# Third pair's last Gram block first, two main-stream fills longer, last row factor by a square root on ScalarE

## The chip, the cores and the metric

The kernel runs on one core of one Trainium2 chip. The metric is the device time of one execution in microseconds (us). Before the change it is 1000.18 us, the median of 3 runs (999.9 to 1000.47).

## The reference, cut to what matters

One layer over 512 tokens with 16 learned tokens ahead of them, 2048 wide, all in float32:

```python
hn = _rmsnorm(h_res, norm_in_g[l])
P = hn @ w_in[l]                        # 2048 x (4224 + 4096)
# first 4224 columns: r, k, v, g_r (1024 each), two low-rank inputs; token-shifted
a = sigmoid(a0 + al @ a_lora_up); decay = exp(-exp(w_raw))
kk = k * k_k, divided by its norm in each head; k = k * (1 + (a - 1) * k_a)
# 16 heads x 64, step by step over the tokens:
S = S * w - (S kk) b^T + v k^T ;  y = S r
y_a = (groupnorm(y) + bonus) * silu(g_r)
# last 4096 columns: Bg, Cg, hc, g_c
y_b = Bg * causal_conv3(Cg * hc) * silu(g_c)
h_res = h_res + concat(y_a, y_b) @ w_out
out = _rmsnorm(h_res, norm_f_g)[:, 16:]
```

The last line is the one that the tail of the kernel computes: every row is scaled by one over the square root of its mean square plus a small constant, and by a gain for each column.

## The kernel before, in words

TensorE (PE) carries the kernel. The projection by `w_in` is a long **main stream** of matmuls (line 328, products `ps_k`, `ps_r`, `ps_v`, `ps_g`, `ps_C`, `ps_h`, `ps_B`, `ps_gc`). Each float32 product is made of three passes, with a coarse and a fine part of the weights (`w`) and of the inputs (`xh`, `xl`): a weight block arrives by DMA (`wr`, line 142), ScalarE (ACT) makes its coarse part (line 134), and VectorE (DVE) or GpSimd (POOL) its fine part (line 135). Weights lie in a ring of six buffers, the two banks of accumulators of the main stream in a ring too.

The state recurrence is done chunk by chunk (9 chunks, 64 tokens each but the first) for eight **pairs** of heads, i = 0 to 7. `prepare(i)` makes a pair's operands: decays and their running sums (`tz`, then the scan `cc`, then `e`), the scaled keys and receptances `bk` and `ar`, squares `sq`, and then the **Gram** matmuls (line 682): for each chunk c and each of two heads, `bk` against `ar`. Their results go to three kinds of accumulators: `za` holds chunks 0 to 3 (names `g_0_0`, `g_0_1` for the two heads in the order of instructions), `zc` chunks 4 to 7 (`g_4_0`, `g_4_1`), and `ze` chunk 8 alone (`g_8_0`, `g_8_1`). `ze` lies in the main stream's own ring of accumulators (tag "main"), so the main product that comes two buffers later can't start before `ze` has been read. DVE reads each by a multiplication with a mask into `gt` (line 692, helper `masked`): a piece of 128x512 for `za` and `zc`, of 128x128 for `ze`. After that the norms of the keys (`n_misc`, `n_tz`, lines 713 and 714) and the bonus sum (`zb`, lines 716 and 717) are computed on PE; `n_misc`, `n_tz` and `zb` take over the banks of `zc` and `za`.

The order on PE is written out by the program: `fill(ns)` places main matmuls, each counted as its columns times 0.43 ns, until `ns` are used up; between two fills stands the next special step. The table `FW` holds these amounts. On the other engines a scheduler of the framework orders the instructions, from the order of the program and its own estimates; an instruction's place on DVE, ACT, POOL and in the DMA queue of SyncE (SP) can move when a step moves on PE.

After the last pair has been solved, `fill(FW["begin"])` comes, and then the recurrence `recur`: it loads the operands of chunk 0 and 1 (`ct` from `opd`, line 936, 15 loads and one) and starts with the matmuls `rz` (line 957).

In the tail the output projection adds its last part to the rows (`end`, matmul line 1449; addition line 1453), ACT squares and sums it (line 1229, an activation and a read of its accumulator), `row_scale` adds the sum to what is there (line 1399) and takes the power -1/2 on POOL (line 98), and `finish_last` scales the four column blocks of the last 128 rows on DVE, ACT and POOL (lines 1418, 1420, 1422, 1423) and sends them out. Rows are handled in four groups t of 128; group 1 is the last.

Of the kernel before, what the change touches and what calls it, by code (L numbers as in the profile page):

```python
# [12 lines left out]
AF = mybir.ActivationFunctionType  # L13
# [12 lines left out]
NCH = SEQ // CH + 1  # L26
# [15 lines left out]

FW = dict(
    evac=34, start=1062, lora=2200, gram=8000, gram_b=13500, gram2=5500, misc=2000, v=2000, vt=1000, solve=24500, solve_first=30000,
    tr=3200, lev=3000, cp=4200, out=1500, begin=20300, p=2900, u=2900, s=4800, last=3700, mix=2600,
)


# [29 lines left out]
def hymba_kernel(ctx: ExitStack, tc: tile.TileContext, xt, xtok, front, w_in, w_out, pv, lup, cst, msk, gf, out):  # L78
    nc = tc.nc
    ctx.enter_context(tc.manual_schedule(engines={mybir.EngineType.PE}))  # L80
    cp = ctx.enter_context(tc.tile_pool(name="cp", bufs=1))
# [12 lines left out]
    def col(off, i=0):  # L94
        return pvt[:, off + i : off + i + 1]

    def rsqrt(y, v):
        nc.gpsimd.tensor_tensor(out=y, in0=v, in1=mhalf[:, 0 : v.shape[1]], op=ALU.pow)
# [198 lines left out]
    with tc.issue_after(head):  # L297
        nc.vector.tensor_scalar(
            out=omm, in0=pvt[:, V_MU : V_MU + 33], scalar1=-1.0, scalar2=1.0, op0=ALU.mult, op1=ALU.add
        )  # L300
        for d, off in (
# [4 lines left out]
                out=d, in0=pvt[:, off : off + 8], scalar1=0.5, scalar2=None, op0=ALU.mult  # L306
            )
        nc.vector.tensor_scalar(
            out=hv[:, 4], in0=pvt[:, V_KA : V_KA + 8], scalar1=-0.5, scalar2=1.0, op0=ALU.mult, op1=ALU.add
# [232 lines left out]
    def step():  # L542
        t = next(flow, None)
        if t is None:
            run_pending(float("inf"))
        else:
            clock[0] += t
            run_pending(clock[0])
        return t

    def fill(ns):
        while ns > 0:
            seen = len(ready)
            t = step()
            if t is None:
                return
            ns -= t
            if len(ready) > seen:
                ns += FW["evac"]
# [26 lines left out]
    def c3(t):  # L586
        return t.rearrange("p (c s) -> p c s", s=CH)
# [39 lines left out]
    def prepare(i):  # L627
        p = i % 2
# [21 lines left out]
            out=bk[:, :, 1], in0=c3(k), scalar=hv[:, 2, i : i + 1], in1=c3(te), op0=ALU.mult, op1=ALU.mult  # L650
        )
        nc.gpsimd.tensor_scalar(
            out=ta, in0=ta, scalar1=hv[:, 3, i : i + 1], scalar2=hv[:, 4, i : i + 1], op0=ALU.mult, op1=ALU.add
        )
        nc.vector.scalar_tensor_tensor(
            out=ar[:, :, 0], in0=c3(k), scalar=col(V_KK, i), in1=e1[:, :, 0:CH], op0=ALU.mult, op1=ALU.mult
# [7 lines left out]
        r = got["r", i]  # L664
        nc.vector.tensor_tensor(
            out=ar[:, 1:NCH, 1], in0=c3(r), in1=e1[:, 1:NCH, 1 : CH + 1], op=ALU.mult
        )
        nc.vector.scalar_tensor_tensor(
            out=r, in0=r, scalar=hv[:, 5, i : i + 1], in1=ta[:, CH:LP], op0=ALU.mult, op1=ALU.mult
# [6 lines left out]
        shift = {0: 2000, 1: 2500, 3: 6000}.get(i, 0)  # L676
# [3 lines left out]
        def gram(z, c, c0):  # L680
            for h, hs, ho in heads:
                nc.tensor.matmul(  # L682
                    z[h][:, c - c0],
                    bk[hs, c, h : h + 2, :].rearrange("p a s -> p (a s)"),
                    ar[hs, c].rearrange("p a s -> p (a s)"),
                    start=True, stop=True,
                )

        def masked(z, c0, c1):
            with ahead():  # L690
                for h in range(2):
                    nc.vector.tensor_tensor(  # L692
                        out=gt[:, h, c0:c1],
                        in0=z[h],
                        in1=gmask[:, h].unsqueeze(1).to_broadcast([P, c1 - c0, P]),
                        op=ALU.mult,
                    )


        za = [pz.tile([P, 4, P], F32, tag="tz", name=f"g{i}_0_{h}") for h in range(2)]  # L700
        zc = [pi.tile([P, 4, P], F32, tag=("misc", "ser")[h], name=f"g{i}_4_{h}") for h in range(2)]
        ze = [pm.tile([P, 1, P], F32, tag="main", name=f"g{i}_8_{h}") for h in range(2)]
        for c in range(NCH):
            gram((za, zc, ze)[c // 4], c, c // 4 * 4)
        for z, a, b in ((ze, 8, 9), (za, 0, 4), (zc, 4, 8)) if i == 2 else ((za, 0, 4), (zc, 4, 8), (ze, 8, 9)):
            masked(z, a, b)
        fill(FW["gram2"] - shift + 1300 * (i == 1) + 2000 * (i == 3))

        n2 = tr(f"n2{i}")
        zn = [pool.tile([2, 288], F32, tag=t, name=f"n2_{i}_{t}") for pool, t in ((pi, "misc"), (pz, "tz"))]  # L710
# [58 lines left out]
        for m in (2, 4, 8):  # L769
            for b in range(16 // (2 * m)):  # L770
# [4 lines left out]
                    out=pq,  # L775
# [5 lines left out]
                    out=tq.rearrange("p (i j) -> p i j", i=m), in_=pq, op=ALU.add, axis=AX.X  # L781
                )
                nc.vector.tensor_tensor(
                    out=pq,
# [30 lines left out]
        v = got["v", i]  # L815
# [245 lines left out]
    for i in range(0, NPAIR, 2):  # L1061
        invert([prepare(i), prepare(i + 1)])
# [9 lines left out]
    mix = [pp.tile([P, 4, SEQ], F32, tag=f"R{m}", name=f"mix{m}") for m in range(4)]  # L1072
# [87 lines left out]
    ssq = pw.tile([P, 92], F32, name="ssq")[:, 0:20].rearrange("p (a b) -> p a b", b=5)  # L1160
    fv = pw.tile([P, 4, 3], F32, name="fv")
# [56 lines left out]
    def here(t, n):  # L1218
        return xa[t][:, n * 512 : (n + 1) * 512] if n < 2 else xb[n - 2][:, t]
# [11 lines left out]
    def gain(t, n, eng, o=slice(0, 512)):  # L1231
        h = here(t, n)[:, o]
        eng.tensor_tensor(out=h, in0=h, in1=gfb[:, n * 512 : (n + 1) * 512][:, o], op=ALU.mult)
# [95 lines left out]
    for half in range(2):  # L1329
        for g in range(4):  # L1330
            b, m1, m2 = U[half, "P5", g], U[half, "M1", g], U[half, "M2", g]
# [39 lines left out]
    z = {}  # L1371
# [17 lines left out]
    def row_part(t, n):  # L1389
        w = fv[:, t, 0:1]  # L1390
        nc.vector.tensor_reduce(out=w, in_=ssq[:, t, 0:n], op=ALU.add, axis=AX.X)
        nc.vector.tensor_scalar(out=w, in0=w, scalar1=RMS_EPS, scalar2=None, op0=ALU.add)

    scales = {}

    def row_scale(t, n, eng=nc.gpsimd):
        f = fv[:, t]
        w, v, r = f[:, 0:1], f[:, 1:2], f[:, 2:3]
        eng.tensor_scalar(out=v, in0=ssq[:, t, n : n + 1], scalar1=w, scalar2=None, op0=ALU.add)
        rsqrt(r, v)  # L1400
        scales[t] = r
# [13 lines left out]
    def finish_last(t):  # L1415
        r = scales[t]
        o = out[t * P : (t + 1) * P]
        nc.vector.tensor_scalar(out=here(t, 2), in0=here(t, 2), scalar1=r, scalar2=1.0, op0=ALU.mult, op1=ALU.mult)
        nc.sync.dma_start(o[:, 1024:1536], here(t, 2))
        nc.scalar.activation(here(t, 0), here(t, 0), AF.Copy, scale=r)  # L1420
        nc.scalar.dma_start(o[:, 0:512], here(t, 0))
        nc.gpsimd.tensor_scalar(out=here(t, 3), in0=here(t, 3), scalar1=r, scalar2=1.0, op0=ALU.mult, op1=ALU.mult)
        nc.vector.tensor_scalar(out=here(t, 1), in0=here(t, 1), scalar1=r, scalar2=1.0, op0=ALU.mult, op1=ALU.mult)
        nc.sync.dma_start(o[:, 512:1024], here(t, 1))
        nc.scalar.dma_start(o[:, 1536:DM], here(t, 3))

    with tc.manual_schedule(engines={mybir.EngineType.DVE, mybir.EngineType.Activation, mybir.EngineType.Pool}):
        end = po.tile([P, 512], F32, tag="o", name="end")
        for g in range(4):
            product((1, "M2", g), [end], (0,))  # L1430
        for t in (2, 3):
            row_part(t, 3)
            row_scale(t, 3)
        row_part(0, 3)
        row_part(1, 3)
        finish(2, (2, 0, 3))
        finish(3, (2,))
        nc.vector.tensor_tensor(out=here(0, 2), in0=here(0, 2), in1=end, op=ALU.add)
        squares(0, 2)
        row_scale(0, 3)  # L1440
        finish(3, (0, 3))
        gain(1, 3, nc.vector)
        ends = [po.tile([P, 256], F32, tag="o", name=f"end{part}") for part in range(2)]
        for part in range(2):
            cols = slice(256 * part, 256 * part + 256)
            for jj in range(8):
                hi, lo = right[(1, "M2", jj // 2), jj % 2]
                for n, (m, w) in enumerate(((0, hi), (0, lo), (1, hi))):
                    nc.tensor.matmul(
                        ends[part], left("M2", jj, m, 1), w[:, cols], start=(jj == 0 and n == 0), stop=(jj == 7 and n == 2)  # L1450
                    )
            h = here(1, 2)[:, cols]
            nc.vector.tensor_tensor(out=h, in0=h, in1=ends[part], op=ALU.add)
            squares(1, 2, part)
            if part == 0:
                gain(1, 2, nc.vector, cols)
                finish(0, (2, 0))
                nc.vector.tensor_tensor(out=fv[:, 1, 0:1], in0=fv[:, 1, 0:1], in1=ssq[:, 1, 3:4], op=ALU.add)
        finish(0, (3,))
        row_scale(1, 4, nc.vector)  # L1460
        gain(1, 2, nc.vector, slice(256, 512))
        finish_last(1)


# [61 lines left out]
```

## Time and profile before

| | |
|---|---|
| median of 3 runs | 1000.18 us (999.9 to 1000.47) |
| the profiled execution's own time | 999.89 us |
| its span | 998.0 us |
| granted TensorE clock, mean | 0.998 |
| busy: PE / DVE / ACT / POOL | 986.7 / 689.2 / 412.2 / 271.6 us |
| DMA moved | 179.48 MB, mean 180 GB/s |

The span is the time that the profiled execution covers; its own time is 1.89 us longer, and the median of the runs is 0.29 us above that. A row of the timeline gives start, duration, engine, line, operation, result and operands, shape and count; in brackets stand the idle time of the engine ahead of it and what ended it. PE is busy nearly all of the time, so the rows to look for are those with a bracket on PE, and those behind its last matmul.

### The profile page before, as it was taken

Reading aid. Unit: us, or ns where it says so; the run is one execution under the profiler, and the core shown is the slowest. Engines: PE = TensorE matmul, PEld = TensorE weight load, DVE = VectorE, ACT = ScalarE, POOL = GpSimd, SP = SyncE. Lnnn points to the kernel's source line nnn. Section 1 sums busy time; section 2 is a strip of 40 time slices with the busy share of each in tenths; the row PEclk is TensorE's granted clock in tenths of the full one; section 3 lists DMA queues with packets and bytes.
Section 4 is the critical chain, followed back from the end, with each engine's and each line's share of the span. In section 5 each row is a group of like instructions: output and inputs, shape, how many; then the busy total and the mean of one; then the engine's idle time right before and its main releaser. Section 6 shows DMA issues by size and latency. Waiting matters only on the chain.

```text
span 998.0 us, 22792 instructions
## 1 busy us (share of the span) xinstructions
PE 986.7 (99%) x9211; PEld 910.8 (91%) x9211; DVE 689.2 (69%) x1314; ACT 412.2 (41%) x770; POOL 271.6 (27%) x286
## 2 busy tenths in 40 slices
PE   9999999999999999999999999999999999999996
PEld 8999999999998999998999998989889898888885
DVE  7777975487774579735579735246555598999895
ACT  7554432343523535232534232233332326645553
POOL 0122423133422324222324222223242423011001
PEclk9999999999999999999999999999999999999999
DMA  9527585437584365854265954978783698798634
GB/s 324 160 79 184 122 224 144 119 106 179 128 215 140 95 180 130 230 145 111 85 180 120 232 143 114 347 266 283 223 266 96 169 266 232 230 293 224 144 99 168
DMA packets 184985, 179.48 MB, mean 180 GB/s; under 512 B 112176, under 2 KB 141616, under 8 KB 184368
## 3 DMA queue, kind: packets, MB, share of 16 engines
q1 hardware_dynamic: 182288, 169.12, 58.2%
q0 software_dynamic: 2304, 8.39, 4.8%
q8 instruction: 72, 1.18, 0.5%
q10 hardware_dynamic: 288, 0.52, 0.1%
q14 instruction: 33, 0.27, 0.1%
HBM read 139.28 MB, written 38.71 MB: 178 GB/s over the span
## 4 chain that ended last, share of the span: by engine, by line
PE 95%; DMA 2%; DVE 1%; issue 1%; POOL 0%; ACT 0%; DVEq 0%; SPq 0%; POOLq 0%
PE ps_g L328 9%; PE ps_r L328 9%; PE ps_h L328 9%; PE ps_gc L328 9%; PE ps_B L328 9%; PE ps_v L328 9%; PE ps_C L328 8%; PE ps_k L328 8%; PE M L1242 8%; PE P L1242 4%; PE Q L1242 2%; PE g L682 2%; DMA ct<-opd 1%; PE ps_lora L328 1%; PE rz L957 1%; PE zs L1004 1%
## 5 line engine op out<-in xcount | busy, mean ns | idle before, releaser
L134 ACT CAST w<-wr 128x512 fp32r<-128x512 f32 x252 | 153.4, 619 | 280.0 <-PE ps_h L328 47.4
L135 POOL TENSOR_TENSOR w<-wr,w 128x512 fp32r<-128x512 f32 x119 | 168.2, 1415 | 365.2 <-ACT w L134 326.7
L135 DVE TENSOR_TENSOR w<-wr,w 128x512 fp32r<-128x512 f32 x133 | 98.3, 743 | 98.6 <-ACT w L134 97.6
L328 PE MATMUL ps_r<-xh,w 128*128 128x256 f32 (+1 forms) x512 | 95.2, 282 | 1.0 <-DVE gt L692 1.0
L328 PE MATMUL ps_k<-xh,w 128*128 128x256 f32 (+1 forms) x512 | 95.4, 284 | 0.0
L328 PE MATMUL ps_v<-xh,w 128*128 128x272 f32 (+1 forms) x512 | 95.4, 284 | 0.0
L328 PE MATMUL ps_h<-xh,w 128*128 128x258 f32 (+1 forms) x512 | 93.1, 281 | 0.0
L328 PE MATMUL ps_C<-xh,w 128*128 128x258 f32 (+1 forms) x512 | 92.5, 281 | 0.0
L328 PE MATMUL ps_g<-xh,w 128*128 128x258 f32 (+1 forms) x512 | 91.7, 280 | 0.0
L328 PE MATMUL ps_B<-xh,w 128*128 128x512 f32 x256 | 83.1, 394 | 0.0
L328 PEld LDWEIGHTS ps_r<-xh,w 128*128 128x128 f32 x512 | 80.2, 189 | 1.6 <-DVE gt L692 1.2
L328 PE MATMUL ps_gc<-xh,w 128*128 128x512 f32 x256 | 81.6, 393 | 0.0
L328 PEld LDWEIGHTS ps_k<-xh,w 128*128 128x128 f32 x512 | 80.3, 189 | 0.3
L328 PEld LDWEIGHTS ps_v<-xh,w 128*128 128x128 f32 x512 | 80.1, 189 | 0.3
L328 PEld LDWEIGHTS ps_h<-xh,w 128*128 128x128 f32 x512 | 79.5, 189 | 0.3
L328 PEld LDWEIGHTS ps_C<-xh,w 128*128 128x128 f32 x512 | 79.2, 189 | 0.6
L328 PEld LDWEIGHTS ps_g<-xh,w 128*128 128x128 f32 x512 | 79.2, 189 | 0.2
L328 PE MATMUL ps_k<-xl,w 128*128 128x256 f32 (+1 forms) x256 | 73.0, 285 | 0.0
L328 PE MATMUL ps_v<-xl,w 128*128 128x256 f32 (+1 forms) x256 | 72.5, 283 | 0.0
L328 PE MATMUL ps_h<-xl,w 128*128 128x256 f32 (+1 forms) x256 | 72.5, 283 | 0.0
L328 PE MATMUL ps_g<-xl,w 128*128 128x256 f32 (+1 forms) x256 | 72.4, 283 | 0.0
L328 PE MATMUL ps_r<-xl,w 128*128 128x256 f32 (+1 forms) x256 | 72.1, 282 | 0.0
(312 smaller groups left out, 2204.3 us busy)
## 6 DMA issues: line engine op xcount, KB each, us to landing
wr<-in_w_in_dram SPq DMA_DIRECT2D x126, 512.0 KB
ct<-opd SPq DMA_DIRECT2D x56, 320.0 KB
wo<-in_w_out_dram SPq DMA_DIRECT2D x21, 512.0 KB
opd<-gt SPq DMA_DIRECT2D x16, 576.0 KB
x<-in_w_out_dram POOLq DMA_DIRECT2D x16, 512.0 KB, 5.7
opd<-ar SPq DMA_DIRECT2D x8, 576.0 KB
opd<-bt SPq DMA_DIRECT2D x64, 64.0 KB
ct<-opd SPq DMA_DIRECT2D x16, 256.0 KB
```

Of the source, the lines that this page charges most:

```text
L134: nc.scalar.copy(hi, rq)
L135: low[q] = eng.tensor_tensor(out=lo, in0=rq, in1=hi.bitcast(F32), op=ALU.subtract).ins
L328: nc.tensor.matmul(ps[r], ww[:, w], xx[:, kt, a:b], start=(kt == 0 and n == 0), stop=(kt == KT - 1 and n == 2))
L682: nc.tensor.matmul(z[h][:, c - c0], bk[hs, c, h : h + 2, :].rearrange("p a s -> p (a s)"), ar[hs, c].rearrange("p a s -> p (a s)"), start= ...
L957: nc.tensor.matmul(z[e][ho if e else hs, 0, k], ct[e][hs, k, o : o + CH], uv(e, k, hs, h) if part else st[hs, 4 * e + k], start=(part == 0 ...
L1004: nc.tensor.matmul(zs[hs, j], bb[:, h], uv(e, k, everything, h), start=True, stop=True)
L1242: nc.tensor.matmul(bank[s], left(prod, jj, m, s), w, start=(jj == 0 and n == 0), stop=(jj == 7 and n == 2))
```

## The change

Four edits:

1. In `prepare`, for the third pair (i = 2), the Gram matmuls of chunk 8 (`ze`) come ahead of those of chunks 0 to 7, and the masks follow the same order. In the program of before, the masks of `ze` stood first for that pair already, and its matmuls last.
2. For the second pair (i = 1), the fill between Gram and norms grows by 400 (1300 to 1700).
3. The fill ahead of the recurrence grows by 500 (20300 to 20800).
4. The factor of the last row group is made by an activation Sqrt on ACT (with the sum as bias) and a reciprocal on DVE, in place of an addition on DVE and a power on POOL. The gain on the second half of the last block is moved ahead of it. After the factors of groups 2 and 3 an activation Sqrt on one element per row is added, whose result isn't used: it stands where the activation table of the square root is to be loaded.

```diff
-    tr=3200, lev=3000, cp=4200, out=1500, begin=20300, p=2900, u=2900, s=4800, last=3700, mix=2600,
+    tr=3200, lev=3000, cp=4200, out=1500, begin=20800, p=2900, u=2900, s=4800, last=3700, mix=2600,
...
-        for c in range(NCH):
-            gram((za, zc, ze)[c // 4], c, c // 4 * 4)
-        for z, a, b in ((ze, 8, 9), (za, 0, 4), (zc, 4, 8)) if i == 2 else ((za, 0, 4), (zc, 4, 8), (ze, 8, 9)):
+        blocks = [(za, 0, 4), (zc, 4, 8), (ze, 8, 9)]
+        if i == 2:
+            blocks = blocks[2:] + blocks[:2]
+        for z, a, b in blocks:
+            for c in range(a, b):
+                gram(z, c, a)
+        for z, a, b in blocks:
             masked(z, a, b)
-        fill(FW["gram2"] - shift + 1300 * (i == 1) + 2000 * (i == 3))
+        fill(FW["gram2"] - shift + 1700 * (i == 1) + 2000 * (i == 3))
...
         w, v, r = f[:, 0:1], f[:, 1:2], f[:, 2:3]
+        if eng is nc.scalar:
+            eng.activation(v, ssq[:, t, n : n + 1], AF.Sqrt, bias=w)
+            nc.vector.reciprocal(r, v)
+            scales[t] = r
+            return
         eng.tensor_scalar(out=v, in0=ssq[:, t, n : n + 1], scalar1=w, scalar2=None, op0=ALU.add)
...
             row_scale(t, 3)
+        nc.scalar.activation(fv[:, 1, 1:2], fv[:, 3, 0:1], AF.Sqrt)
         row_part(0, 3)
...
-        row_scale(1, 4, nc.vector)
         gain(1, 2, nc.vector, slice(256, 512))
+        row_scale(1, 4, nc.scalar)
```

Lines below the third edit of the file are numbered 4 higher in the changed program (713 becomes 717), and 9 or 10 higher in the tail (1229 becomes 1233, 1409 becomes 1418).

**Second pair, PE.** On PE around the norms (`n_`) and the bonus sum (`zb`) of the second pair, before the change:

```order
L328 MATMUL ps_g_1_1652<-xh,w_1482 128x258 x2
L713 MATMUL n_1_misc<-sq_h,ones 2x288
L714 MATMUL n_1_misc<-sq_l,ones 2x288
L713 MATMUL n_1_tz<-sq_h,ones 2x288
L714 MATMUL n_1_tz<-sq_l,ones 2x288
L716 MATMUL zb_1798<-rk_h,ones 128x512
L717 MATMUL zb_1798<-rk_l,ones 128x512
L328 MATMUL ps_g_1_1652<-xl,w_1482 128x258
L328 MATMUL ps_g_1_1652<-xh,w_1482 128x258
L328 MATMUL ps_C_0_1825<-xh,w_1545 128x256
```

and after it:

```order
L328 MATMUL ps_g_1_1652<-xh,w_1482 128x258 x2
L328 MATMUL ps_g_1_1652<-xl,w_1482 128x258
L328 MATMUL ps_g_1_1652<-xh,w_1482 128x258
L328 MATMUL ps_C_0_1812<-xh,w_1545 128x256
L328 MATMUL ps_C_0_1812<-xl,w_1545 128x256
L717 MATMUL n_1_misc<-sq_h,ones 2x288
L718 MATMUL n_1_misc<-sq_l,ones 2x288
L717 MATMUL n_1_tz<-sq_h,ones 2x288
L718 MATMUL n_1_tz<-sq_l,ones 2x288
L720 MATMUL zb_1823<-rk_h,ones 128x512
```

Four main matmuls have moved ahead of the norms, two of them already of the next product, `ps_C`.

**Third pair, DVE.** On DVE from the product `bk` (line 659) of the third pair to the mask of `g_8_0`, before (the masks of `g_4_1` and `g_8_1` follow; the subtraction `sq_l`, line 602, stands three rows ahead of the first row):

```order
L659 TENSOR_TENSOR bk_2657<-ta_2738,e_2816 128x9x64
L135 TENSOR_TENSOR w_2795<-wr_2793,w_2795 128x512
L668 SCALAR_TENSOR_TENSOR r_2624<-r_2624,hv,ta_2738 128x512
L729 STREAM_TRANSPOSE bt_3062<-bk_2657 128x512 x2
L602 TENSOR_TENSOR rk_l<-r_2624,rk_h 128x512
L821 STREAM_TRANSPOSE vs_3136<-v_2781 128x576
L135 TENSOR_TENSOR w_2858<-wr_2856,w_2858 128x512
L692 TENSOR_TENSOR gt_2919<-g_0_0_2920,cs 128x512
L692 TENSOR_TENSOR gt_2919<-g_0_1_2921,cs 128x512
L692 TENSOR_TENSOR gt_2919<-g_4_0_2922,cs 128x512
L692 TENSOR_TENSOR gt_2919<-g_8_0_2924,cs 128x128
```

and after:

```order
L659 TENSOR_TENSOR bk_2661<-ta_2742,e_2820 128x9x64
L135 TENSOR_TENSOR w_2795<-wr_2793,w_2795 128x512
L668 SCALAR_TENSOR_TENSOR r_2582<-r_2582,hv,ta_2742 128x512
L602 TENSOR_TENSOR sq_l<-sq_2834,sq_h 128x576
L733 STREAM_TRANSPOSE bt_3066<-bk_2661 128x512
L602 TENSOR_TENSOR rk_l<-r_2582,rk_h 128x512
L733 STREAM_TRANSPOSE bt_3066<-bk_2661 128x512
L825 STREAM_TRANSPOSE vs_3140<-v_2781 128x576
L135 TENSOR_TENSOR w_2858<-wr_2856,w_2858 128x512
L692 TENSOR_TENSOR gt_2923<-g_8_0_2928,cs 128x128
L692 TENSOR_TENSOR gt_2923<-g_8_1_2929,cs 128x128
L692 TENSOR_TENSOR gt_2923<-g_0_0_2924,cs 128x512
```

The mask of `g_8_0` has moved from the fourth place of the six to the first; and `sq_l`, which stood ahead of `bk`, now stands between `bk` and the masks. On POOL, ahead of that, the scaling of `tz` (line 639), on which the scan and everything after it rests, stands so before:

```order
L358 MEMSET pr_k_2969 128x1
L639 TENSOR_SCALAR tz_2675<-tz_2675 128x576
L135 TENSOR_TENSOR w_2637<-wr_2632,w_2637 128x512
L661 COPY dd<-e_2658 128x9
L642 MEMSET e_3150 128x9
```

and so after:

```order
L358 MEMSET pr_k_2969 128x1
L135 TENSOR_TENSOR w_2595<-wr_2590,w_2595 128x512
L639 TENSOR_SCALAR tz_2687<-tz_2687 128x576
L661 COPY dd<-e_2662 128x9
L642 MEMSET e_3154 128x9
```

The fine part of a weight block has moved ahead of `tz`. It is the block whose coarse part ACT makes behind its part of `tz` before (second half, line 578) and ahead of it after. On PE the Gram matmuls of this pair stand four main matmuls later than before.

**Recurrence, PE and SP.** The matmuls `rz` stand four main matmuls later than before; the loads of `ct` on SP keep their order and their neighbours.

**Tail, ACT and DVE.** On ACT, from the sums of squares of the first part (`sqj` of groups 3 and 1) on, after the change:

```order
L1233 ACTIVATE sqj_3_None,ssq<-xb_11533 128x512
L1233 ACTIVATE sqj_1_None,ssq<-xb_11533 128x512
L1443 ACT_TABLE_LOAD
L1443 ACTIVATE fv<-fv 128x1
L1233 ACTIVATE sqj_2_None,ssq<-xb_11508 128x512
L1421 ACTIVATE xa_11037<-xa_11037,fv 128x1024
```

This ACT_TABLE_LOAD is the only one besides the one at the start of the program (line 246), which before has alone; the sum of squares of group 2 follows it. At the end of DVE's program stand, before:

```order
L1453 TENSOR_TENSOR xb_11508<-xb_11508,end_12273 128x256
L1409 SCALAR_TENSOR_TENSOR xb_11533<-xb_11533,fv,gfb 128x512
L1399 TENSOR_SCALAR fv<-ssq,fv 128x1
L1300 TENSOR_TENSOR xb_11508<-xb_11508,gfb 128x256
L1418 TENSOR_SCALAR xb_11508<-xb_11508,fv 128x512
```

and after:

```order
L1463 TENSOR_TENSOR xb_11508<-xb_11508,end_12274 128x256
L1418 SCALAR_TENSOR_TENSOR xb_11533<-xb_11533,fv,gfb 128x512
L1304 TENSOR_TENSOR xb_11508<-xb_11508,gfb 128x256
L1405 RECIPROCAL fv<-fv 128x1
L1427 TENSOR_SCALAR xb_11508<-xb_11508,fv 128x512
```

The addition has left DVE, and the reciprocal stands between the gain and the last scalings.

## The prediction

> **What bounds the kernel now.** I read the page first: the busy times and the chain that ended last.
>
> ```profile
> PE 986.7 (99%) x9211; PEld 910.8 (91%) x9211; DVE 689.2 (69%) x1314; ACT 412.2 (41%) x770; POOL 271.6 (27%) x286
> PE 95%; DMA 2%; DVE 1%; issue 1%; POOL 0%; ACT 0%; DVEq 0%; SPq 0%; POOLq 0%
> ```
>
> PE is busy 986.7 of 998.0 us, and the change takes no matmul away. So there are only 11.3 us to win from, and the next view, PE's waits by what ended them, tells how much of that is waiting in the middle.
>
> ```profile
> PE ps_r L328 <- DVE gt L692: 1.0, 1, 1.0
> PE rz L957 <- DMA ct<-opd: 0.3, 1, 0.3
> ```
>
> Two of the edits aim at these two waits. The third wait that I look for is in PE's weight loads, and the last stretch begins where PE stops, at 989.83 + 0.28 = 990.11, 7.9 us before the end:
>
> ```profile
> 130.60 0.19 PEld L716 LDWEIGHTS zb<-rk_h,ones 128*128 128x128 f32 x1 [0.43 <-issue]
> 989.83 0.28 PE L1449 MATMUL end<-home,m 128*128 128x256 f32 x1
> ```
>
> All sums below go against the profiled execution, 999.89 us; the median of the runs, 1000.18, lies 0.29 above it, and I add this back at the end. A measurement of this kernel can tell about 0.2%, 2.0 us, from no change.
>
> **Third pair (edit 1).** The timeline of PE and DVE around the third pair's Gram:
>
> ```profile
> 214.60 2.28 PE L682 MATMUL g<-ar,bk 64*128 64x128 f32 x36
> 218.74 0.28 PE L328 MATMUL ps_k<-xl,w 128*128 128x272 f32 x1
> 218.87 0.29 PE L328 MATMUL ps_k<-xh,w 128*128 128x272 f32 x1
> 220.11 0.38 PE L328 MATMUL ps_r<-xh,w 128*128 128x256 f32 x1 [0.96 <-DVE gt L692]
> 217.99 2.87 DVE L692 TENSOR_TENSOR gt<-g,cs 128x512 f32<-128x512 f32 x6
> ```
>
> Main matmuls start 0.12 to 0.13 apart (218.74, 218.87), so `ps_r` was due at 218.99 and came at 220.11: **1.12 us** lost. It takes over the buffer of `ze`, whose mask is the fourth of the six: 217.99 plus three pieces of some 0.6 plus its own 0.27 is 220.06. Put first, that mask would end at 218.26, before 218.99, and all 1.12 would go. But DVE doesn't reach it at the same time as before:
>
> ```profile
> 198.43 0.48 ACT L578 ACTIVATE tz<-tz,hv 128x256 f32<-128x256 f32 x1 [1.53 <-PE tz L572]
> 198.98 0.62 ACT L134 CAST w<-wr 128x512 fp32r<-128x512 f32 x1
> 199.07 1.67 POOL L639 TENSOR_SCALAR tz<-tz 128x576 f32<-128x576 f32 x1 [3.21 <-ACT tz L578]
> 200.70 1.30 POOL L135 TENSOR_TENSOR w<-wr,w 128x512 fp32r<-128x512 f32 x1
> 209.31 1.86 DVE L658 TENSOR_TENSOR ta<-ta,k 128x576 f32<-128x576 f32 x1 [0.26 <-POOL ta L652]
> 211.09 0.74 DVE L602 TENSOR_TENSOR sq_l<-sq,sq_h 128x576 fp32r<-128x576 f32 x1
> 212.57 0.75 DVE L659 TENSOR_TENSOR bk<-ta,e 128x576 f32<-128x576 f32 x1
> 213.35 0.67 ACT L660 COPY bk<-bk 64x576 f32<-64x576 f32 x1 [2.85 <-DVE bk L659]
> ```
>
> By the order of instructions, the weight block's cast stands ahead of ACT's `tz` now and the block's fine part ahead of POOL's. The cast waits for a weight buffer that PE frees about where it freed it before, at some 198.9; then 0.62 for the cast, 1.30 for the fine part, and `tz` starts on POOL near 200.8 instead of 199.07: **1.75 late**. What of that reaches `bk` at line 659? Along the way 0.1 to 0.2 goes in idle time of DVE, and `sq_l`, which stood ahead of `bk`, no longer does (0.74, some 0.07 of it beside its neighbours). I take 0.8 late: `bk` at 213.35, ACT's copy done at 214.8. The Gram matmuls stand four main matmuls later, at 214.60 + 0.47 = 215.07, so they are covered by about 0.3 us.
>
> From `bk` to the first mask it took 217.99 - 212.57 = 5.42 us. Now `sq_l` lies in this stretch, +0.67. One step there was stretched before:
>
> ```profile
> 213.24 0.68 DVE L135 TENSOR_TENSOR w<-wr,w 128x512 fp32r<-128x512 f32 x1
> 216.98 1.08 DVE L135 TENSOR_TENSOR w<-wr,w 128x512 fp32r<-128x512 f32 x1
> 215.92 1.60 POOL L135 TENSOR_TENSOR w<-wr,w 128x512 fp32r<-128x512 f32 x1 [4.55 <-ACT w L134]
> ```
>
> The same operation takes 0.68 alone and 1.08 beside POOL's, which ran to 217.52; moved to about 218.3 it runs behind POOL's, -0.41. The first mask then starts at 213.35 + 5.42 + 0.67 - 0.41 = 219.03 and ends at 219.3, and `ps_r` waits some 0.35 instead of 1.12: **0.75 won**. Bounds: if the delay of `bk` is only 0.4 and POOL is out of the way, 1.1; if `bk` is 1.0 late and the two meet again, the mask ends at 219.9 and 0.2 is left. I take 0.75, nearest to the chain of rows.
>
> The Trainium skill ("SBUF — State Buffer", the section "SBUF: two separate sides") says that a DVE instruction with two SBUF inputs and a GpSimd instruction that reads SBUF exclude each other, whichever starts first. The trace agrees: behind 217.52 DVE's step had 0.54 left. By that rule a meeting would cost up to the whole rest of POOL's 1.30, and the term could fall to about zero; by the rows it fell by 0.4.
>
> **Second pair (edit 2).**
>
> ```profile
> 127.82 2.86 DVE L692 TENSOR_TENSOR gt<-g,cs 128x512 f32<-128x512 f32 x6
> 130.21 0.29 PE L714 MATMUL n_tz<-sq_l,ones 128*2 128x288 f32 x1
> 130.63 0.47 PE L716 MATMUL zb<-rk_h,ones 128*128 128x512 f32 x1
> ```
>
> `zb` follows `n_tz` by 0.42, where matmuls of this width start 0.13 apart, and its weight load was idle for 0.43: 0.29 lost. `zb` takes over the bank of `g_4_1`, the fifth mask, which ends at 127.82 + 2.0 + 0.67 = 130.49. With four main matmuls (0.47) ahead of the norms, `zb` is due at 130.81, 0.3 behind that. But `ps_C` now starts ahead of the norms, at 130.06, in the buffer of `g_8_0`, the fourth mask, done at 127.82 + 1.8 + 0.27 = 129.89: covered by 0.17. **0.29 won** (0 to 0.29).
>
> **Recurrence (edit 3).**
>
> ```profile
> 630.97 0.81 PE L957 MATMUL rz<-ct 64*64 64x64 f32 x28
> 632.11 0.33 PE L957 MATMUL rz<-ct 64*64 64x64 f32 x4 [0.33 <-DMA ct<-opd]
> ```
>
> The last load of chunk 0 landed 0.33 after PE wanted it. Four main matmuls more ahead of `rz` give 0.47, while the loads keep their place on SP behind the same weight load, which waits for a buffer that PE frees; so they keep their distance to PE. **0.33 won** (0.1 to 0.33, since the cover is only 0.14).
>
> **Tail (edit 4).**
>
> ```profile
> 2.03 0.20 ACT L246 ACTIVATE warm<-warm 128x1 f32<-128x1 f32 x1
> 990.98 0.19 ACT L1229 ACTIVATION_READ_ACCUMULATOR sqj<-xb 128x1 f32 x1
> 991.20 0.21 DVE L1399 TENSOR_SCALAR fv<-ssq,fv 128x1 f32<-128x1 f32 x1
> 991.33 0.41 DVE L1300 TENSOR_TENSOR xb<-xb,gfb 128x256 f32<-128x256 f32 x1
> 991.49 0.66 POOL L98 TENSOR_TENSOR fv<-fv,mhalf 128x1 f32<-128x1 f32 x1 [4.33 <-DVE fv L1399]
> 992.19 0.72 ACT L1420 ACTIVATE xa<-xa,fv 128x512 f32<-128x512 f32 x1 [1.02 <-POOL fv L98]
> L757 DVE RECIPROCAL nd<-nd x8: 249/249/251, 95.5 to 562.8; 72x16 f32<-72x16 f32 x8
> ```
>
> Now the square root follows the read at 991.17 on the same engine: 0.20 by the small activation, 0.3 with an allowance of 0.1, done by 991.5. The gain takes 0.41 from 991.20 on. The reciprocal starts near 991.6 and takes at most the 0.25 that 16 columns take, at least the 0.15 or so of a small step: done at 991.75, and the scalings start at 991.78 instead of 992.19. **0.42 won** (0.2 to 0.6).
>
> The price is the second table load. It lies here:
>
> ```profile
> 0.73 1.28 ACT L246 ACT_TABLE_LOAD   x1 [0.73 <-PEq L1513]
> 979.01 0.63 ACT L1229 ACTIVATE sqj_None<-xb 128x512 f32<-128x512 f32 x1 [1.07 <-DVE xb L1223]
> 985.18 0.63 ACT L1229 ACTIVATE sqj_None<-xb 128x512 f32<-128x512 f32 x1 [2.57 <-DVE xb L1438]
> 987.78 0.42 ACT L1229 ACTIVATE sqj<-xb 128x256 f32<-128x256 f32 x1 [0.84 <-DVE xb L1453]
> ```
>
> 1.28 + 0.20 go into an idle time of 1.07, so groups 2 and 3 run 0.4 to 0.5 late; the idle times of 2.57 and 0.84 behind them take that up before PE's last part, 987.27. Cost nothing; without this cover it would be 0.45.
>
> The Trainium skill ("ScalarE: Activation LUTs", the section "What ACT_TABLE_LOAD costs") counts a drain of about 1.38 us with each load, 2.66 in all. The one load in this trace shows 1.28 and the next instruction 0.02 behind it, but it had nothing to drain. By the page's price groups 2 and 3 would run 1.8 late and the last sum some 0.3: the tail would win 0.1, and the whole 0.3 less.
>
> **The sum.** 0.75 + 0.29 + 0.33 + 0.42 = 1.79. 999.89 - 1.8 = 998.1 for a profiled execution; 1000.18 - 1.8 = **998.4** for the median.
>
> **The rivals.**
> *All waits go* (the third pair's chain is hardly late): 1.1 + 0.29 + 0.33 + 0.45 = 2.2, 998.0. For it speaks that DVE and ACT have idle time in that chain; against it the 1.75 at its head.
> *The third pair stays as it was*: `bk` is later than I think. At over 1.05 late the Gram itself waits (copy done 214.02 + 1.05 = 215.07). With the whole 1.75 passed on and `sq_l` behind it, the mask ends at 218.26 + 1.75 + 0.67 = 220.7: the place loses 0.6 instead of winning, and the time is 1000.18 - 1.04 + 0.6 = 999.7. The head of the chain speaks for it; `sq_l` ahead of `bk`, which is gone, against it.
> *Slower: the second pair's solve starves.* Its divisors `nd` are now loaded from SP behind the 576 KB of `ar`, and DVE has the gating `g` ahead of them.
>
> ```profile
> 161.33 0.64 SPq L796 DMA_DIRECT2D xo<-sx  x1
> 171.64 0.70 DVE L845 STREAM_TRANSPOSE xn<-xT 128x512 f32<-128x512 f32 x1
> ```
>
> The solve's start is read back from DRAM by loads whose last is issued at 161.97; with an allowance of 2 to 3 for its landing and 171.64 for its use, some 7 us of cover are there. The delay is 576 KB at the page's mean of 180 GB/s, 3.3 us. From 7 on PE waits for each us; at 8.8 all is lost, and at 10.8 the kernel is 2 us slower, 1002.2. The distance speaks against it.
> *Edits 2 and 3 only move the waits* (`ps_C` waits for its mask, the `ct` loads come later by as much): 1.17 is won, 999.0.
>
> **How the numbers follow.** My forecast with its bounds has 0.50, all waits gone 0.17, the third pair unchanged or worse 0.15, moved waits 0.10, the slower case 0.08. The range is 997.6 to 999.9: from all waits gone with 0.6 in the tail, to the third pair's loss. Faster by over 0.2% means under 998.18: the first rival's 0.17, and 0.17 of the forecast's 0.50, together 0.34. Slower by over 0.2%: 0.08. Within: 0.58.
>
> **What would show it.** After: `ps_r` of the fourth pair with a bracket of about 0.2 to 0.4 for `gt`, POOL's `tz` some 1.7 us later against PE, no bracket on `g`; `zb` 0.13 behind `n_tz` in the second pair and none on `ps_C`; no bracket on `rz`; the last scalings 1.67 us behind PE's last matmul instead of 2.08. A new bracket on PE anywhere else, above all where the shifts of up to five main matmuls leave other steps earlier or later, would make me wrong, as would a table load longer than 1.9 us.

## The result, and the profile after

The changed kernel takes **997.8 us** (median of 12 runs, 997.26 to 998.39) against 1000.2 us for the kernel before, measured beside it (12 runs, 998.8 to 1000.79). The ratio is 0.9978 (95% interval 0.9971 to 0.9985), so 1.5 to 2.9 us were won. Measured again on another occasion the ratio was 0.9983 (0.9974 to 0.9991). The forecast was 998.4, a gain of 1.8.

The profiled execution took 998.33 us with a span of 996.5 (before: 999.89 and 998.0). The waits of PE after the change, by what ended them, are these two; both waits that were to go are gone, and one is new:

```profile
PE pwarm L187 <- DVE cold L184: 1.4, 1, 1.4
PE tz L571 <- DVE xT L923: 0.3, 1, 0.3
```

**Second pair.** PE, timeline: `zb` follows `n_tz` by 0.14 instead of 0.42, and the matmuls of `ps_C` ahead of the norms have no bracket.

```profile
130.33 0.33 PE L328 MATMUL ps_C<-xh,w 128*128 128x256 f32 x1
131.00 0.30 PE L718 MATMUL n_tz<-sq_l,ones 128*2 128x288 f32 x1
131.14 0.40 PE L720 MATMUL zb<-rk_h,ones 128*128 128x512 f32 x1
```

**Third pair.** PE and DVE after the change: `ps_r` follows `ps_k` by 0.12, so all of the 1.12 is gone. The masks begin at 218.05, both masks of `ze` are done by 218.52 (0.47 for the two), and `ps_r` was due at 219.27 and came then.

```profile
215.35 2.28 PE L682 MATMUL g<-ar,bk 64*128 64x128 f32 x36
219.15 0.29 PE L328 MATMUL ps_k<-xh,w 128*128 128x272 f32 x1
219.27 0.28 PE L328 MATMUL ps_r<-xh,w 128*128 128x256 f32 x1
217.47 0.64 DVE L135 TENSOR_TENSOR w<-wr,w 128x512 fp32r<-128x512 f32 x1
218.05 2.86 DVE L692 TENSOR_TENSOR gt<-g,cs 128x128 f32<-128x128 f32 x6
```

That is 1 us earlier than I had worked out (219.03), though the head of the chain came as late as I had said, and a little more. POOL and DVE after:

```profile
199.77 1.29 POOL L135 TENSOR_TENSOR w<-wr,w 128x512 fp32r<-128x512 f32 x1 [5.41 <-ACT w L134]
201.03 1.66 POOL L639 TENSOR_SCALAR tz<-tz 128x576 f32<-128x576 f32 x1
202.73 1.36 DVE L641 TENSOR_TENSOR_SCAN cc<-smask,tz 128x576 f32<-128x576 f32 x1 [5.44 <-POOL tz L639]
212.39 0.75 DVE L659 TENSOR_TENSOR bk<-ta,e 128x576 f32<-128x576 f32 x1
```

and the scan before, with the second pair's ahead of it:

```profile
100.48 2.43 DVE L641 TENSOR_TENSOR_SCAN cc<-smask,tz 128x576 f32<-128x576 f32 x1 [0.44 <-POOL tz L639]
200.78 2.43 DVE L641 TENSOR_TENSOR_SCAN cc<-smask,tz 128x576 f32<-128x576 f32 x1 [3.81 <-POOL tz L639]
```

POOL's `tz` came 1.96 later (201.03 against 199.07). But before the change POOL's weight step at 200.70 ran beside the scan and stretched it to 2.43 us; now that step lies ahead of `tz`, and the scan takes 1.36. The second pair's scan is the only other long one, and it too has a weight step of POOL beside it (100.41, 1.29 long). In all fourteen profiles every scan with such a step beside it takes 2.43 or 2.44, and every other one 1.34 to 1.36. The move gave 1.07 back at once. Another 0.40 was made up on the way to the step ahead of `bk` (line 658), and 0.67 because `sq_l` no longer lies ahead, so that `bk` came 0.18 earlier than before by the clock, not 0.8 later. From `bk` to the first mask it took 5.66, close to the 5.68 worked out.

**The new wait** lies ahead of all this, at the low-rank matmul of the third pair. PE and DVE after, then PE and DVE before:

```profile
195.44 0.40 PE L328 MATMUL ps_v<-xh,w 128*128 128x256 f32 x2
196.10 0.36 PE L571 MATMUL tz<-la,luh 128*128 128x272 f32 x1 [0.26 <-DVE xT L923]
192.96 1.25 DVE L372 SCALAR_TENSOR_TENSOR r<-pr_r,omm,sh_r 128x512 f32<-128x512 f32 x1 [0.84 <-ACT sh_r L371]
194.13 2.43 DVE L923 COPY xT<-z 32x128 f32<-32x128 f32 x8
```

```profile
195.25 0.29 PE L328 MATMUL ps_v<-xh,w 128*128 128x272 f32 x1
195.38 0.29 PE L571 MATMUL tz<-la,luh 128*128 128x272 f32 x1
192.52 2.40 DVE L919 COPY xT<-z 32x128 f32<-32x128 f32 x8 [0.22 <-PE z L913]
194.95 0.76 DVE L372 SCALAR_TENSOR_TENSOR r<-pr_r,omm,sh_r 128x512 f32<-128x512 f32 x1
```

DVE now makes `r` before it copies the solve's results out of the bank (`xT<-z`), and `tz`, which takes that bank over, waits for the copies. Counted from start to start, `tz` came 0.54 behind the last matmul of `ps_v` (195.44 + 0.12, then 196.10) where 0.12 to 0.13 is due: 0.42 lost, more than the bracket of 0.26.

**Recurrence.** `rz` runs through in one piece:

```profile
630.69 0.69 PE L961 MATMUL rz<-ct 64*64 64x64 f32 x32
```

From the last main matmul ahead of it to the first behind it 0.83 us pass, where it was 1.62 in the execution before. So that execution had lost 0.79 there, not the 0.33 of the bracket: 28 of the 32 matmuls stood under one row of 0.81 that already held some of the waiting.

**Tail.** ACT and DVE after:

```profile
975.85 1.28 ACT L1443 ACT_TABLE_LOAD   x1
977.25 0.62 ACT L1233 ACTIVATE sqj_None<-xb 128x512 f32<-128x512 f32 x1
989.26 0.19 ACT L1233 ACTIVATION_READ_ACCUMULATOR sqj<-xb 128x1 f32 x1
989.48 0.29 ACT L1404 ACTIVATE fv<-ssq,fv 128x1 f32<-128x1 f32 x1
989.82 0.16 DVE L1405 RECIPROCAL fv<-fv 128x1 f32<-128x1 f32 x1
990.01 0.72 ACT L1429 ACTIVATE xa<-xa,fv 128x512 f32<-128x512 f32 x1 [0.24 <-DVE fv L1405]
```

PE's last matmul ends at 988.39, 1.72 earlier than before, and the scalings start 1.62 behind it instead of 2.08. But from there to the end of the span it takes 996.5 - 990.01 = 6.49 us, where it took 998.0 - 992.19 = 5.81. The 0.46 won was given back, and 0.22 more. What lay there was the question of the last three experiments.

### The profile page after: what moved, and what is told of

Same layout as the page of the kernel before. It is cut to its first block, busy times and chain, and to the rows that moved or that the text cites. A ratio compares the mean times of both kernels' runs of the same rounds, so it can differ in the third digit from the quotient of the medians.

```text
span 996.5 us, 22799 instructions
## 1 busy us (share of the span) xinstructions
PE 986.5 (99%) x9211; PEld 911.1 (91%) x9211; DVE 686.7 (69%) x1314; ACT 413.4 (41%) x773; POOL 268.2 (27%) x285
## 4 chain that ended last, share of the span: by engine, by line
PE 98%; DVE 1%; ACT 0%; issue 0%; DVEq 0%; ACTq 0%
PE ps_k L328 9%; PE ps_h L328 9%; PE ps_r L328 9%; PE ps_C L328 9%; PE ps_g L328 9%; PE ps_gc L328 9%; PE ps_v L328 9%; PE ps_B L328 9%; PE M L1246 8%; PE P L1246 4%; PE Q L1246 2%; PE g L682 2%; PE ps_lora L328 1%; PE rz L961 1%; PE zs L1008 1%; PE zy L1012 1%
## 5 line engine op out<-in xcount | busy, mean ns | idle before, releaser
L328 PE MATMUL ps_C<-xl,w 128*128 128x256 f32 (+1 forms) x256 | 71.9, 281 | 0.0
```

Source lines behind the costliest of these rows:

```text
L328: nc.tensor.matmul(ps[r], ww[:, w], xx[:, kt, a:b], start=(kt == 0 and n == 0), stop=(kt == KT - 1 and n == 2))
```

## The experiments

One table first. All numbers are from PE's timeline, start to start, less what the same step takes without a wait (0.13 for `zb`, 0.12 for `tz` and `ps_r`, 0.83 for the first `rz` block), and at the end the two stretches behind PE's last matmul. All in us.

| kernel | zb | tz | ps_r | rz | PE's end to scalings | scalings to end |
|---|---|---|---|---|---|---|
| before | 0.29 | 0.01 | 1.12 | 0.79 | 2.08 | 5.81 |
| changed | 0.01 | 0.42 | 0 | 0 | 1.62 | 6.49 |
| e1_gram | 0.31 | 0 | 0 | 0.47 | 2.08 | 5.80 |
| e2_norms | 0 | 0.41 | 0.88 | 0.57 | 2.09 | 5.83 |
| e3_begin | 0.31 | 0 | 1.12 | 0.20 | 2.08 | 5.84 |
| e4_tail | 0.31 | 0.01 | 1.11 | 0.01 | 1.63 | 6.09 |
| after_again | 0 | 0.42 | 0 | 0.01 | 1.62 | 6.55 |
| e5_no_norms | 0.29 | 0 | 0 | 0 | 1.63 | 6.07 |
| e6_given_back | 0 | 0.01 | 0 | 0.04 | 1.63 | 6.53 |
| e8_begin_more | 0 | 0.01 | 0 | 0.01 | 1.63 | 6.37 |
| e7_no_warm | 0 | 0.43 | 0 | 0 | 2.89 | 6.13 |

The measured times are less sharp than these rows. In the eleven profiles of the table the first `ps_g` matmul, which lies ahead of every edit, starts anywhere from 104.34 to 105.61, because the start of the kernel varies. That alone is more than any one term.

**Each edit alone.** The four parts, each put into the kernel before:

```diff
--- before
+++ e1_gram
...
+        if i == 2:
+            blocks = blocks[2:] + blocks[:2]
+        for z, a, b in blocks:
+            for c in range(a, b):
+                gram(z, c, a)
...
--- before
+++ e2_norms
-        fill(FW["gram2"] - shift + 1300 * (i == 1) + 2000 * (i == 3))
+        fill(FW["gram2"] - shift + 1700 * (i == 1) + 2000 * (i == 3))
--- before
+++ e3_begin
-    tr=3200, lev=3000, cp=4200, out=1500, begin=20300, p=2900, u=2900, s=4800, last=3700, mix=2600,
+    tr=3200, lev=3000, cp=4200, out=1500, begin=20800, p=2900, u=2900, s=4800, last=3700, mix=2600,
--- before
+++ e4_tail
...
+            eng.activation(v, ssq[:, t, n : n + 1], AF.Sqrt, bias=w)
+            nc.vector.reciprocal(r, v)
...
+        nc.scalar.activation(fv[:, 1, 1:2], fv[:, 3, 0:1], AF.Sqrt)
...
-        row_scale(1, 4, nc.vector)
         gain(1, 2, nc.vector, slice(256, 512))
+        row_scale(1, 4, nc.scalar)
```

> Edit 1 alone (third pair: chunk 8's Gram matmuls and masks first). Theory A: the wait of 0.3 at the third pair's low-rank matmul (tz) after the change comes from edit 2, not from this one. Then here DVE copies xT ahead of r as before, POOL's tz isn't late, the first mask ends near 218.3, and ps_r follows ps_k by 0.12 instead of 1.24: PE is 1.1 us earlier from there to the end, 999.1 by the clock of before (1000.2). Theory B: putting chunk 8 first itself brings the late chain: a bracket of about 0.3 on tz, and only 0.8 won, 999.4.

Measured: ratio 0.9983 (0.9974 to 0.9992), and no new wait. Theory A: the wait at `tz` doesn't come from this edit, and alone it takes the whole 1.12. POOL's `tz` isn't late here, its weight step still lies beside the scan, and the scan takes 2.44; the masks come in time all the same.

```profile
218.01 0.29 PE L328 MATMUL ps_k<-xh,w 128*128 128x272 f32 x1
218.14 0.28 PE L328 MATMUL ps_r<-xh,w 128*128 128x256 f32 x1
```

> Edit 2 alone (second pair's fill 1300 to 1700). Theory A: zb follows n_tz by 0.13 instead of 0.42 (0.29 won), but DVE then has r ahead of the copies xT in the solve, PE waits about 0.3 for xT at the third pair's tz, and POOL's tz is late, so that the mask of chunk 8, still fourth, ends later or the same: the sum is 0.0, or up to 0.5 lost, 1000.2 to 1000.7. Theory B: the wait at tz belongs to edit 1: 0.29 won, 999.9.

Measured: ratio 0.9993 (0.9984 to 1.0002). The wait at `tz` is there, with DVE in the new order: `r` at 192.94, the copies at 194.12. So edit 2 wins 0.29 and loses 0.41. POOL's new order is edit 2's as well: the weight step stands ahead of `tz` here too, and the third pair's scan takes 1.36. The masks still come in the old order, but the wait of `ps_r` falls to 0.88, not up as I had feared.

```profile
196.08 0.36 PE L571 MATMUL tz<-la,luh 128*128 128x272 f32 x1 [0.26 <-DVE xT L919]
192.94 1.25 DVE L372 SCALAR_TENSOR_TENSOR r<-pr_r,omm,sh_r 128x512 f32<-128x512 f32 x1 [0.84 <-ACT sh_r L371]
194.12 2.43 DVE L919 COPY xT<-z 32x128 f32<-32x128 f32 x8
220.13 0.38 PE L328 MATMUL ps_r<-xh,w 128*128 128x256 f32 x1 [0.71 <-DVE gt L692]
```

> Edit 3 alone (fill ahead of the recurrence 20300 to 20800). Theory A: the first rz block takes 0.83 from the last main matmul ahead of it to the first behind it, instead of 1.62, so 0.8 is won, 999.4; the bracket of 0.33 showed only the part of the loss behind the modelled end of the matmuls. Theory B: the bracket was the loss, 0.33 is won, 999.9, and the other 0.5 of the changed kernel comes from elsewhere.

Measured: ratio 0.9990 (0.9982 to 0.9999). The `rz` block takes 1.03, with 0.20 still lost. Theory A was right that the bracket understates the loss of one execution, but not that 0.8 is there to win each time: in `e4_tail`, which doesn't touch this place, the block ran through in 0.84. The row of `e3_begin`, then that of `e4_tail`:

```profile
631.09 0.90 PE L957 MATMUL rz<-ct 64*64 64x64 f32 x32
631.33 0.69 PE L957 MATMUL rz<-ct 64*64 64x64 f32 x32
```

> Edit 4 alone (last row factor by a square root on ScalarE). Theory A: the last scalings start 1.62 us behind PE's last matmul instead of 2.08: 0.46 won, 999.7, and groups 2 and 3 run at most 0.2 late. Theory B: the second table load costs more than it shows, by a drain: 0.1 won at most, 1000.1.

Measured: ratio 0.9999 (0.9990 to 1.0008). The scalings start 1.63 behind PE's end, as theory A has it, but the end of the span is 6.09 behind them instead of 5.81. Neither theory had that.

Taken by their ratios, the four edits alone would win 1.7, 0.7, 1.0 and 0.1 us, 3.5 together, where the whole change wins 2.2. Each ratio is only good to some 0.9 us, so the times can't weigh the terms against each other, and the rows have to.

**Is the wait at `tz` edit 2's, and can it be had without?**

```diff
--- changed
+++ e5_no_norms
-        fill(FW["gram2"] - shift + 1700 * (i == 1) + 2000 * (i == 3))
+        fill(FW["gram2"] - shift + 1300 * (i == 1) + 2000 * (i == 3))
--- changed
+++ e6_given_back
-        fill(FW["misc"])
+        fill(FW["misc"] - 400 * (i == 1))
--- e6_given_back
+++ e8_begin_more
-    tr=3200, lev=3000, cp=4200, out=1500, begin=20800, p=2900, u=2900, s=4800, last=3700, mix=2600,
+    tr=3200, lev=3000, cp=4200, out=1500, begin=21300, p=2900, u=2900, s=4800, last=3700, mix=2600,
```

> The changed kernel once more, beside the next three. Both theories: 2.2 us below the kernel before (997.8 where that has 1000.2). Theory A: the gap ahead of the third pair's tz is 0.54 again where 0.13 is due, and rz takes 0.83 to 1.0; theory B (the wait at tz was chance): the gap is 0.13 this time.

Measured: 0.9983 (0.9974 to 0.9991), and 0.42 lost at `tz` again. It isn't chance.

> Edits 1, 3 and 4 without edit 2. Theory A: zb loses its 0.3 again, the gap ahead of tz is back at 0.13 (0.41 won), POOL's tz isn't late, so 0.1 faster than the whole change: 997.7. Theory B (edit 2 is a plain gain, the wait at tz belongs to edit 1): 0.3 slower than the whole change, 998.1, with the gap of 0.54 at tz.

Measured: 0.9979 (0.9970 to 0.9987). `tz` has no wait, `zb` has lost its 0.29 again, and POOL's `tz` is in its old place. In time it can't be told from the changed kernel, so edit 2 has no gain that shows.

> The whole change, and the four matmuls that edit 2 puts ahead of the second pair's norms are taken out of the next fill behind them (misc 2000 to 1600 for that pair), so that everything behind stands where it stood before. Theory A: zb 0.13 behind n_tz and the gap ahead of tz 0.13: 0.4 faster than the whole change, 997.4. Theory B: the gap stays at 0.54 or another wait takes its place, 997.8.

Measured: 0.9979 (0.9970 to 0.9987). Both waits are gone: DVE copies `xT` ahead of `r` again, and `zb` follows `n_tz` directly. In time this can't be told from the changed kernel beside it: 997.90 against 997.92, and not the 0.4 less that theory A had. In the two profiles the 0.42 saved at `tz` is lost at the block of `z` matmuls in the first solve, behind the second pair (1.80 against 1.29 in `after_again`), so that from the first `ps_g` to the end of its last matmul PE takes 882.75 here and 882.69 there.

```profile
194.91 0.29 PE L571 MATMUL tz<-la,luh 128*128 128x272 f32 x1
192.04 2.40 DVE L923 COPY xT<-z 32x128 f32<-32x128 f32 x8 [0.22 <-PE z L917]
194.47 0.75 DVE L372 SCALAR_TENSOR_TENSOR r<-pr_r,omm,sh_r 128x512 f32<-128x512 f32 x1
```

> The kernel with four matmuls given back, and four more matmuls ahead of the recurrence (begin 21300). The time from the last main matmul ahead of rz to the first behind it was 1.62, 1.40, 1.30 and 0.84 in four runs with the old fill, 0.83 and 1.03 in two with the new one. Theory A (the loads of ct land at times that differ by some 0.8 from run to run): it is 0.83 here, and the median is 0.1 below that of the kernel with four matmuls given back, 997.3. Theory B (the loads are behind a fixed distance that the change already covers): no difference, 997.4, or worse where the later start makes later steps wait.

Measured: 0.9979 (0.9971 to 0.9988); `rz` loses 0.01. Over all the profiles `rz` lost 0.79, 0.47, 0.57 and 0.01 with the old fill (and 0.33 and 0.41 in the two kernels below that have it), 0, 0.01, 0.20, 0, 0.04, 0 and 0 with the new one. So the edit is worth 0.4 in the mean, and the larger fill adds nothing that shows.

**The price of the table load.**

```diff
--- changed
+++ e7_no_warm
-        nc.scalar.activation(fv[:, 1, 1:2], fv[:, 3, 0:1], AF.Sqrt)
```

> The whole change without the activation that loads the square root's table early, so the load stands between the last sum of squares and the last square root. Theory A: it costs the 1.28 that its row shows and nothing more: the last scalings start 1.62 + 1.3 = 2.9 us behind PE's last matmul, 999.1. Theory B (a drain of 1.4 us with each load, the price of 2.66 in the Trainium skill, ScalarE: Activation LUTs, the section What ACT_TABLE_LOAD costs): 4.3 behind it, 1000.5.

Measured: ratio 0.9988 (0.9978 to 0.9997), 998.9 us. The scalings start 2.89 behind PE's end, 1.27 later than in the changed kernel. The profiled execution is the slowest of this kernel's ten (1001.17), with 1.1 us of waits at the matmuls `M` ahead of the tail, so only its single rows are used, not its total. ACT at the end:

```profile
991.25 0.19 ACT L1233 ACTIVATION_READ_ACCUMULATOR sqj<-xb 128x1 f32 x1
991.45 1.28 ACT L1404 ACT_TABLE_LOAD   x1
992.75 0.29 ACT L1404 ACTIVATE fv<-ssq,fv 128x1 f32<-128x1 f32 x1
```

The load starts 0.01 behind the read's end and the square root 0.02 behind the load's: 1.28 and no drain. The 1.38 that the Trainium skill ("ScalarE: Activation LUTs", the section "What ACT_TABLE_LOAD costs") adds to it doesn't appear here.

**Where the tail's gain went.** In the changed kernel the last 4 us of the span, as 40 slices of 0.1 us of what the DMA engines moved, and the queue that only the kernels with edit 4 have there; after:

```profile
GB/s 389 389 348 348 430 369 369 389 348 389 430 348 369 369 369 430 144 0 41 20 0 20 0 0 0 0 0 0 0 0 0 0 0 0 0 0 0 0 0 0
q14 instruction: 1, 0.01, 0.5%
```

and before, where q14 has no row:

```profile
GB/s 348 410 328 287 451 410 389 369 389 369 430 348 389 369 389 389 430 328 389 348 369 410 307 103 0 0 0 0 0 0 0 0 0 0 0 0 0 0 0 0
```

Before, the transfers end together. After, the bulk ends and single packets straggle behind it for half a microsecond. An instruction fetch has moved in among the last output transfers: in all seven kernels with edit 4 in the table it lies 1.75 to 3.5 us ahead of the end of the span, in the four without that edit 0.5 to 1.25 us behind it. The stretch from the scalings to the end goes with its place: 6.07 to 6.13 in the three kernels where the fetch lies 1.75 to 2 us ahead of the end, 6.37 to 6.55 in the four where it lies 2.5 to 3.5 ahead. Two ways to test that:

```diff
--- before
+++ e9_three_more
         finish(3, (2,))
+        for _ in range(3):
+            nc.scalar.activation(fv[:, 1, 1:2], fv[:, 3, 0:1], AF.Copy)
```

`e11_seven_more` is the same with 7; `e10_twelve_more` is `e6_given_back` with 12 of them at the same place.

> The kernel before, and three one-element-per-row copies more in ScalarE's program, in an idle time of the tail (no square root, no table load). From the start of the last scalings to the end of the span the kernels without edit 4 take 5.80 to 5.84 us, those with it 6.07 to 6.55, and only in those lies an instruction fetch (queue q14) inside the span, 1.75 to 3.5 us before its end. Theory F (ScalarE's longer program draws its next fetch into the last output transfers, and these end later for it): 6.1 to 6.6 here too, with the fetch inside, 1000.4. Theory G (the square root or the table load itself delays the end): 5.8 and no fetch inside, 1000.0.

Measured: 1.0004 (0.9995 to 1.0013); 5.97 from the scalings to the end, and the fetch 0.5 behind the end. A miss: with three copies the fetch lies no earlier than in `e2_norms`, which has none of them, so it isn't inside, and this run tells nothing about either theory. More of them were needed.

> The kernel before with seven one-element-per-row copies more on ScalarE in the tail, instead of three (with three the fetch came 0.5 us after the end of the span, before it 1.25 after: not drawn in). Theory F: with seven the fetch lies inside the last transfers, 1.5 to 3.5 us before the end, and from the last scalings to the end it takes 6.1 to 6.6 instead of 5.8, without any square root: 1000.5. Theory G (edit 4's instructions themselves): 5.8 to 6.0 wherever the fetch lies, 1000.0.

Measured: 1.0008 (0.9999 to 1.0018). The fetch is inside, 3.5 ahead of the end, and the stretch takes 998.0 - 991.56 = 6.44, without a square root or a table load in the tail; from PE's end to the scalings it is 2.08, as before. In time alone the loss isn't clear of noise. ACT's scaling, and the DMA engines in the last 4 us, which show the same straggling packets:

```profile
991.56 0.72 ACT L1420 ACTIVATE xa<-xa,fv 128x512 f32<-128x512 f32 x1 [1.02 <-POOL fv L98]
GB/s 369 471 369 328 348 471 389 389 369 328 369 348 410 430 348 369 266 62 21 20 41 20 0 0 0 0 0 0 0 0 0 0 0 0 0 0 0 0 0 0
q14 instruction: 1, 0.01, 0.5%
```

> The kernel with the four matmuls given back (all edits in it), and twelve such copies more on ScalarE in the idle time of 2.6 us ahead of the squares of group 0. Theory F: the fetch comes twelve instructions earlier in ScalarE's program, before the last transfers, and from the last scalings to the end it takes 5.8 again, with 1.6 from PE's last matmul to the scalings: some 0.5 faster than without the copies, 997.4. Theory G: 6.1 to 6.6 as before, 997.9.

Measured: **996.77 us** against 999.91, ratio 0.9968 (0.9958 to 0.9977), the fastest of all kernels here, though the interval overlaps that of `e6_given_back` (0.9970 to 0.9987). The fetch lies 8.5 ahead of the end, before the last outputs, and from the scalings to the end it takes 995.1 - 989.21 = 5.89 instead of 6.53; the transfers end together again:

```profile
989.21 0.72 ACT L1429 ACTIVATE xa<-xa,fv 128x512 f32<-128x512 f32 x1 [0.24 <-DVE fv L1405]
GB/s 389 328 328 348 451 430 369 369 348 369 410 410 369 389 369 410 369 389 369 389 348 348 185 0 0 0 0 0 0 0 0 0 0 0 0 0 0 0 0 0
```

Theory F holds in both directions, with one profile each: the fetch put in without edit 4 lengthens the end by 0.6, and edit 4 without the fetch there keeps its gain. Why the fetch moves as far as it does with edit 4's few instructions stays open: they bring it from 0.5 to 1.25 behind the end to 1.75 to 3.5 ahead of it, where three copies don't move it by anything that shows.

## Why the prediction was right, and where it was not

The total was right: 1.8 won against 2.2 (1.5 to 2.9) and 1.7 (0.9 to 2.6). Of its four terms one holds as it was worked out, two come out in size for other reasons than given, and one is lost. So the agreement of the total is partly luck.

- **Second pair, 0.29.** Right in size and in its place: the 0.28 to 0.31 lost without the edit is at most 0.01 with it. What I missed is that the edit reaches further. The four matmuls also shift the first solve's end, where the scheduler then lets DVE make `r` before it copies `xT`. I had read the order of instructions from the third pair's `tz` on, not ahead of it. With the 0.42 at `tz` counted against it, the edit as a whole wins nothing.
- **Third pair, 0.75.** The sum at this pair is 1.12 - 0.42 = 0.70, by two errors that cancel, which is luck. By edit it divides otherwise: edit 1 wins the whole 1.12, and the late `tz` on POOL, which I had worked out under edit 1, comes with edit 2. The step that failed is "What of that reaches `bk`": I took 0.8 of the 1.75 as late. The runs showed 1.96 at its head, and 1.07 of it given back by the scan, whose row of 2.43 I had on the table but took for its own duration; six of the eight pairs' scans take 1.34 to 1.36, and the two of 2.43 are those with a step of POOL beside them. That a step of POOL holds up one of DVE, which I had weighed at one row, was at work at this one as well. So the masks weren't late, the whole 1.12 went, and the 0.42 at `tz` went the other way.
- **Recurrence, 0.33.** About right in the mean (0.4), wrong as a reading. The bracket of 0.33 was the part of a loss of 0.79 that lay behind the modelled end of the matmuls, and that loss varies from profile to profile: 0.01 to 0.79 in six profiles with the old fill. The bracket names the loads of `ct`; why they land so differently stays open.
- **Tail, 0.42.** The step that failed is the sum's last: I let the gain at the scalings stand for a gain at the end. The scalings did come 0.46 earlier, and the table load was hidden as worked out (group 2's squares 1.41 us behind the read before them, instead of 1.06). But the fetch lengthened the end by 0.3 to 0.7, so the edit's net effect lies between 0.2 won and 0.3 lost.
- **The rivals.** *All waits go* (2.2, 998.0) came nearest: its condition, that the third pair's chain is hardly late, is what the rows show, and the three waits went. What it lacked is the new wait at `tz` and the longer end. The third pair was not left as it was; no starved solve showed; the waits didn't just move at edits 2 and 3. "A new bracket on PE anywhere else" is what came, from the shift that I had named and not followed.

Between the two profiled executions the terms add up. From the first `ps_g` to the end of PE's last matmul it took 885.04 us before and 883.06 after, 1.98 less. The four waits give 0.28 + 1.12 - 0.41 + 0.79 = 1.78 of that, and the block of `z` matmuls in the first solve, behind the second pair (line 870 before), the rest, 1.80 against 1.57. The kernel after started this stretch 0.26 later and took 0.22 longer behind it, so its span is 1.5 shorter.

In the mean over the profiles, 0.29 + 0.70 + 0.4 - 0.2, the terms come to 1.2, less than the 2.2 measured and below its interval. Part of the difference may lie at that block of `z`: it takes 1.3 in some profiles and up to 2.0 in others, 1.36 in the mean of the four kernels with edit 2 and nothing given back, 1.68 in the mean of the ten others. The profile shows nothing that ends this idle time but "issue", and two kernels without the edit have 1.31 as well; what decides it stays open.

## What to carry to other kernels

Where a step is moved, look at the rows that it leaves as well as at those that it meets: an operation that is longer than its fellows of the same shape may owe it to the very step that goes. Take the loss at a wait from start to start of the neighbours and from several profiles, not from one bracket. And count a gain at the end only where the last transfer lands, with the instruction fetches among what can delay it.

## What the runs showed of the hardware

- One instruction fetch of 0.01 MB among the last output transfers made single packets trail and the span 0.3 to 0.7 us longer (6.07 to 6.55 against 5.80 to 5.84 from the scalings to the end); twelve one-element copies more on ACT, which bring it earlier, took that away (5.89).
- A scan of 128x576 on DVE took 2.43 us beside a 1.30 us step of POOL with two inputs, and 1.36 alone: it took 1.07 longer for the 1.22 that the two overlapped. All fourteen profiles agree.
- A table load on ACT between two dependent steps cost its 1.28 us and nothing more.
- The start of the kernel varied by 1.3 us from profile to profile (first `ps_g` at 104.34 to 105.61), without any bracket on PE that tells why in most of them.
